# A last down projection of which 22 of 88 contraction tiles are made, two by two, by seven products of sums in place of eight, with their weight blocks on GpSimd's queue

## The chip, the cores and the metric

The kernel runs on one core of one Trainium2 chip. The metric is the time of one execution on the device in microseconds (us). A core has TensorE (PE, matrix products out of SBUF into PSUM), VectorE (DVE), ScalarE (ACT), GpSimd (POOL) and SyncE (SP), each with its own stream of instructions, and 16 DMA engines, for which SP, ACT and POOL issue transfers on a queue each.

## What is computed

A decoder trunk on one sequence of 256 tokens and 2048 features: a conformer convolution layer with its SwiGLU, a layer of dilated attention with its SwiGLU, and a final normalisation. The change touches only the end:

```python
h = h + _swiglu(_rmsnorm(h, ffn_norm_g[layer]), ffn_w_gate[layer], ffn_w_up[layer], ffn_w_down[layer])
return _rmsnorm(h, final_norm_g)      # (silu(x @ w_gate) * (x @ w_up)) @ w_down, w_down: 5632 x 2048, float32
```

## The kernel before

All work is on tiles of 128 partitions. Activations stand transposed (features on partitions, 256 tokens along the row), `hT` holds the residual. Each weight is float32 and each float32 product is made as three products of a faster type: a weight block is split into `whi` (a rounded copy, ScalarE, line 176) and `wlo` (the rest, VectorE, line 178), each activation likewise, and high x high, high x low and low x high are added up in PSUM.

Weight blocks of 512 KB come in the order of the list `blocks`. `next_block` (line 183) hands out the next one and first writes the instructions of the blocks up to two ahead (`emit_block`, line 153): the load into one of three `raw` buffers on SP's queue (line 173), then copy and subtraction into one of four `whi` and four `wlo` buffers. The order of instructions on each engine is laid out by a planner from the written order and the times that it expects; `later(n, fn)` writes `fn` after n further blocks, counted by `tick`.

The last down projection (lines 730 to 788) is token-major: `project_nat` (line 293) takes for each of four column blocks c (512 columns) the 22 blocks of 2 contraction tiles each. A block is multiplied with two halves of the tokens (t = 0, 1; 128 each), which are the stationary operand, the weights the moving one: 2 x 2 x 3 = 12 matmuls of 128 x 512, into one PSUM bank for each t. PSUM has eight banks: `pp` is two pairs, `aux` three banks, `one` one bank. During the first eight blocks of the stage `turn_over` (line 742) transposes the residual with `ident` (a part of the constants in `cst`), and ScalarE copies it into `hn`. At the end of a column block `add` (line 753) adds it to the residual and sums the squares, GpSimd multiplies by the gain. In the last column block the last three blocks are taken first for t = 0, then for t = 1, so that `done` (line 772: root, reciprocal, scaling and stores of the output) of the first half of the tokens runs beside the products of the second.

Of the kernel before, what the change touches and what calls it, by code (L numbers as in the profile page):

```python
# [9 lines left out]
F32 = mybir.dt.float32  # L10
F32R = mybir.dt.float32r
AF = mybir.ActivationFunctionType
ALU = mybir.AluOpType
# [3 lines left out]
P = 128  # L17
# [17 lines left out]
NATIVE = 4  # L35

TAPS_OF = [(6, 0)] * 14 + [(6, 6), (3, 16)]


_VEC = {}  # L40
# [39 lines left out]
def trunk(ctx: ExitStack, tc: tile.TileContext, xT, vec, const, w1, w2, wk, wv, wq, wo, wg0, wu0, wd0, wg1, wu1, wd1, fing, out):  # L80
# [34 lines left out]
    def new_x(pool, name, n=DT):  # L115

        return pool.tile([P, n, 2, S], F32R, name=name)
# [4 lines left out]
    def plan(w, u, kt_n, gk=GK):  # L122
        blocks.extend((w, u, g, gk) for g in range(kt_n // gk))
# [9 lines left out]
    for wg, wu, wd in ((wg0, wu0, wd0), (wg1, wu1, wd1)):  # L133
        for u in range(FT // 2):
            plan(wg, u, DT)
            plan(wu, u, DT)
        if wd is wd1:
            for c in range(D // NBV):
                plan(wd, c, FT, GKV)
# [10 lines left out]
    conv_pool = []  # L150
   

    def emit_block():
        i = len(ready)
        w, u, g, gk = blocks[i]
# [24 lines left out]
        if with_x and g == DT // GK - 1:  # L180
            x_loaded()

    def next_block(w, u, g, ahead=AHEAD):
        i = used[0]
        used[0] += 1
        assert blocks[i][:3] == (w, u, g)
        while len(ready) < min(len(blocks), i + 1 + ahead):
            emit_block()
        return ready[i]
# [42 lines left out]
    def bank2():  # L232
        return psum[-1].tile([P, 2, 2, S], F32, name="pp", bufs=2)

    def aux(shape):
        return psum[-1].tile(shape, F32, name="aux", bufs=3 if len(psum) > 1 else 5)
# [53 lines left out]
                                             skip_group_check=True)  # L290
                yield

    def project_nat(w, c, x, kt_n=DT, done=None):


        n = kt_n // GKV
        held = AHEAD + 1 if done else 0
        if done:
            outs = [aux([P, NBV]) for _ in range(2)]
        else:  # L300
            bk = bank2()
            outs = [bk[:, t, :, :].rearrange("p a b -> p (a b)") for t in range(2)]

        def tiles(hi, lo, g, j, t):
            kt = g * GKV + j
            o = outs[t]
            ts = slice(t * P, (t + 1) * P)
            nc.tensor.matmul(o, x[:, kt, 0, ts], hi[:, j, :], start=kt == 0, stop=False)  # L308
            nc.tensor.matmul(o, x[:, kt, 0, ts], lo[:, j, :], start=False, stop=False)  # L309
            nc.tensor.matmul(o, x[:, kt, 1, ts], hi[:, j, :], start=False, stop=kt == kt_n - 1)  # L310

        for g in range(n - held):
            hi, lo = next_block(w, c, g)[1:]
            for j in range(GKV):
                for t in range(2):
                    tiles(hi, lo, g, j, t)
            tick()
        last = []
        for t in range(2) if done else ():
            for g in range(n - held, n):  # L320
                if t == 0:
                    last.append(next_block(w, c, g)[1:])
                for j in range(GKV):
                    tiles(*last[g - n + held], g, j, t)
            done(t, outs[t])
        return outs

    def collect(bk, pool, name, bufs):
# [401 lines left out]
    with tc.tile_pool(name="ff", bufs=1) as ff:  # L730
        hid = ffn_hidden(ff, wg1, wu1, x, norm)
        table(AF.Sqrt, silu[-1])

        both = new_x(rp, "x").bitcast(F32).rearrange("p t a s -> p (t a s)").rearrange("p (i t n) -> p i t n", i=2, t=2)
        hn, on = both[:, 0, :, :], both[:, 1, :, :]
        ss = [little("ss", 8) for t in range(2)]
        gain = []
        for c in range(D // NBV):
            gain.append(ff.tile([P, 2, S], F32, name="t", bufs=4).rearrange("p a b -> p (a b)"))
            nc.scalar.dma_start(gain[c], fing[:, c * NBV:(c + 1) * NBV])  # L740

        def turn_over(i, t):

            pt = aux([P, 4, P])
            for a in range(4):
                nc.tensor.transpose(pt[:, a, :], hT[:, 4 * i + a, t * P:(t + 1) * P], ident)
            nc.scalar.copy(hn[:, t, 4 * i * P:4 * (i + 1) * P], pt.rearrange("p a b -> p (a b)"))

        for i in range(DT // 4):
            for t in range(2):  # L750
                later(2 * i + t, lambda i=i, t=t: turn_over(i, t))

        def add(c, t, p):

            cs = slice(c * NBV, (c + 1) * NBV)
            nc.vector.tensor_tensor(out=hn[:, t, cs], in0=p, in1=hn[:, t, cs], op=ALU.add)
            nc.vector.scalar_tensor_tensor(out=on[:, t, cs], in0=hn[:, t, cs], scalar=1.0, in1=hn[:, t, cs], op0=ALU.mult, op1=ALU.mult,
                                           accum_out=ss[t][:, c:c + 1])
            if c < D // NBV - 1:
                nc.gpsimd.tensor_tensor(out=on[:, t, cs], in0=hn[:, t, cs], in1=gain[c], op=ALU.mult)  # L760

        for c in range(D // NBV - 1):
            bk = project_nat(wd1, c, hid, FT)
            for t in range(2):
                add(c, t, bk[t])

        for t in range(2):
            r = ss[t][:, 4:5]
            nc.vector.tensor_reduce(out=r, in_=ss[t][:, 0:3], axis=AX.X, op=ALU.add)
            nc.vector.tensor_scalar(out=r, in0=r, scalar1=1.0 / D, scalar2=RMS_EPS, op0=ALU.mult, op1=ALU.add)  # L770

        def done(t, p):
            c = D // NBV - 1
            add(c, t, p)
            r = ss[t][:, 5:6]
            nc.scalar.activation(r, ss[t][:, c:c + 1], AF.Sqrt, scale=1.0 / D, bias=ss[t][:, 4:5])
            nc.vector.reciprocal(r, r)
            for i, eng in ((0, nc.scalar), (2, nc.vector), (1, nc.scalar), (3, nc.vector)):
                cs = slice(i * NBV, (i + 1) * NBV)
                if i == c:  # L780
                    nc.vector.scalar_tensor_tensor(out=on[:, t, cs], in0=hn[:, t, cs], scalar=r, in1=gain[c], op0=ALU.mult, op1=ALU.mult)
                elif eng is nc.scalar:
                    nc.scalar.activation(on[:, t, cs], on[:, t, cs], AF.Identity, scale=r)
                else:
                    nc.vector.tensor_scalar(out=on[:, t, cs], in0=on[:, t, cs], scalar1=r, scalar2=None, op0=ALU.mult)
                (nc.scalar if eng is nc.scalar else nc.sync).dma_start(out[t, :, cs], on[:, t, cs])

        project_nat(wd1, D // NBV - 1, hid, FT, done)


def _rows(a):
# [44 lines left out]
```

## Time and profile before

| what | value |
|---|---|
| median of 3 runs | 2182.6 us (2182.5 to 2182.79) |
| profiled execution: its own time | 2182.09 us |
| profiled execution: span from first to last instruction | 2180.3 us |
| granted TensorE clock, mean | 0.998 of full speed |
| TensorE busy | 2161.6 us (99% of the span) |
| last down projection on TensorE | from 1929.47 us to the last matmul at 2172.47 us |

A line of the timeline gives start, duration, engine, line of the kernel, operation, and the tiles written and read. Matmuls are pipelined: a duration reaches past the start of the next one, so what one costs is read from start to start. PE and PEld are matmul and the load of the stationary operand, which overlap. A buffer number is left out of a tile's name.

### The profile page before, as it was taken

The numbers are of one execution on the slowest core, as the hardware profiler recorded it, in microseconds if no ns is written. First come the engines' busy times: TensorE is split into PE (matmuls) and PEld (weight loads), VectorE is DVE, ScalarE is ACT, GpSimd is POOL, SyncE is SP. The second block draws the span as 40 slices with busy tenths as digits, with TensorE's granted clock in tenths as the row PEclk, the third lists the DMA queues.
The fourth block names the chain that finished last, engine by engine and source line by source line (L and its number), as shares of the span: only waits on it lengthen the run. The fifth ranks groups of instructions, "written<-read, shape, count | busy, mean of one in ns | idle before, by whom it ended". The sixth has DMA issues, their size and how long they took to land.

```text
span 2180.3 us, 31164 instructions
## 1 busy us (share of the span) xinstructions
PE 2161.6 (99%) x12254; PEld 1904.8 (87%) x12254; DVE 1327.9 (61%) x1636; ACT 1063.1 (49%) x1385; POOL 418.2 (19%) x284
## 2 busy tenths in 40 slices
PE   9999899999999999999999999999999999999998
PEld 8999788888888888888888888888888888888887
DVE  6888866555555554555545777665555555545554
ACT  6665555444444443444444566454444444453333
POOL 5998111111121210000000100012121111200000
PEclk9999999999999999999999999999999999999999
DMA  7444355555555555555565544555555555565564
GB/s 248 175 167 162 106 194 183 190 187 193 192 187 191 186 192 190 188 193 192 184 193 191 188 143 146 177 191 186 190 188 191 192 189 188 193 198 192 194 193 160
DMA packets 112899, 402.42 MB, mean 185 GB/s; under 512 B 12656, under 2 KB 13680, under 8 KB 112752
## 3 DMA queue, kind: packets, MB, share of 16 engines
q1 hardware_dynamic: 111456, 398.30, 55.1%
q8 instruction: 96, 1.57, 0.3%
q10 hardware_dynamic: 1296, 2.12, 0.3%
q14 instruction: 51, 0.42, 0.1%
HBM read 398.28 MB, written 2.10 MB: 184 GB/s over the span
## 4 chain that ended last, share of the span: by engine, by line
PE 97%; DVE 1%; DMA 1%; ACT 0%; issue 0%; POOL 0%; SPq 0%; ACTq 0%; DVEq 0%; POOLq 0%
PE pp L222 47%; PE pp L226 25%; PE pp L264 7%; PE pp L308 4%; PE pp L310 4%; PE pp L309 4%; PE aux L310 1%; PE aux L308 1%; PE aux L309 1%; PE pp L289 1%; DMA raw<-w 0%; DVE aux L475 0%; PE pp L277 0%; PE aux L700 0%; PE aux L677 0%
## 5 line engine op out<-in xcount | busy, mean ns | idle before, releaser
L178 DVE TENSOR_TENSOR wlo<-raw,whi 128x1024 fp32r<-128x1024 f32 (+1 forms) x692 | 900.8, 1318 | 752.7 <-ACT whi L176 598.1
L176 ACT CAST whi<-raw 128x1024 fp32r<-128x1024 f32 (+1 forms) x737 | 771.1, 1048 | 951.6 <-PE pp L222 633.8
L222 PE MATMUL pp<-x,whi 128*128 128x512 f32 x3328 | 778.0, 390 | 0.0
L222 PEld LDWEIGHTS pp<-x,whi 128*128 128x128 f32 x3328 | 617.2, 188 | 123.4
L226 PEld LDWEIGHTS pp<-x,wlo 128*128 128x128 f32 x3328 | 414.2, 192 | 8.6
L226 PE MATMUL pp<-x,wlo 128*128 128x256 f32 x3328 | 418.6, 283 | 0.0
L222 PE MATMUL pp<-hid,whi 128*128 128x512 f32 x704 | 164.3, 390 | 0.0
L222 PEld LDWEIGHTS pp<-hid,whi 128*128 128x128 f32 x704 | 130.6, 188 | 26.1
L475 DVE SCALAR_TENSOR_TENSOR aux<-up,vecs,aux 128x256 f32<-128x256 f32 x350 | 140.9, 481 | 1.6 <-ACT aux L473 1.6
L655 POOL TENSOR_TENSOR hid<-t,hid 128x512 fp32r<-128x512 f32 x44 | 57.1, 1298 | 417.1 <-ACT hid L654 417.1
L264 PE MATMUL pp<-x,whi 128*128 128x256 f32 x720 | 133.5, 287 | 0.0
L360 POOL TENSOR_TENSOR sqacc<-sqacc,sq 128x512 f32<-128x512 f32 x22 | 29.5, 1343 | 516.3 <-ACT sq L356 506.1
L649 POOL TENSOR_TENSOR t<-t,rstd 128x512 f32<-128x512 f32 x44 | 57.1, 1298 | 344.3 <-DVE t L332 344.3
L264 PEld LDWEIGHTS pp<-x,whi 128*128 128x128 f32 x720 | 113.3, 192 | 0.9
L178 POOL TENSOR_TENSOR wlo<-raw,whi 128x1024 fp32r<-128x1024 f32 x45 | 107.2, 2407 | 21.3 <-ACT whi L176 21.3
L308 PE MATMUL pp<-whi,hid 128*128 128x512 f32 x264 | 103.5, 392 | 0.0
L310 PE MATMUL pp<-whi,hid 128*128 128x512 f32 x264 | 102.8, 390 | 0.0
L309 PE MATMUL pp<-wlo,hid 128*128 128x512 f32 x264 | 102.8, 389 | 0.0
L264 PE MATMUL pp<-x,wlo 128*128 128x256 f32 x360 | 101.8, 283 | 0.0
L331 ACT COPY t<-pp 128x512 f32<-128x512 f32 x104 | 61.2, 589 | 71.7 <-PE pp L222 71.7
L226 PEld LDWEIGHTS pp<-hid,wlo 128*128 128x128 f32 x704 | 87.6, 192 | 1.9
L226 PE MATMUL pp<-hid,wlo 128*128 128x256 f32 x704 | 88.2, 283 | 0.0
(156 smaller groups left out, 1960.1 us busy)
## 6 DMA issues: line engine op xcount, KB each, us to landing
raw<-wg SPq DMA_DIRECT2D x176, 512.0 KB, 3.3
raw<-wu SPq DMA_DIRECT2D x176, 512.0 KB, 3.3
raw<-wd SPq DMA_DIRECT2D x176, 512.0 KB, 3.9
raw<-w SPq DMA_DIRECT2D x75, 512.0 KB, 3.3
raw<-wv SPq DMA_DIRECT2D x32, 512.0 KB, 4.2
raw<-wk SPq DMA_DIRECT2D x32, 512.0 KB, 3.4
raw<-wq SPq DMA_DIRECT2D x32, 512.0 KB, 3.2
raw<-wo SPq DMA_DIRECT2D x32, 512.0 KB, 3.3
```

The costliest lines, as they stand in the source:

```text
L176: nc.scalar.copy(hi[:, part, :], raw[:, part, :])
L178: eng.tensor_tensor(out=lo[:, part, :], in0=raw[:, part, :], in1=hi[:, part, :].bitcast(F32), op=ALU.subtract)
L222: nc.tensor.matmul(bk[:, m, :, :], hi, x[:, k, :, :], start=k == 0, stop=k == kt_n - 1 and turned, skip_group_check=True)
L226: nc.tensor.matmul(bk[:, m, 0, :], lo, x[:, k, 0, :], start=False, stop=k == kt_n - 1 and not turned, skip_group_check=True)
L264: nc.tensor.matmul(bks[u][:, m, :], a[:, j, m * P:(m + 1) * P], b, start=kt == 0 and m == 0 and i == 0, stop=kt == DT - 1 and i == len(pas ...
L308: nc.tensor.matmul(o, x[:, kt, 0, ts], hi[:, j, :], start=kt == 0, stop=False)
L309: nc.tensor.matmul(o, x[:, kt, 0, ts], lo[:, j, :], start=False, stop=False)
L310: nc.tensor.matmul(o, x[:, kt, 1, ts], hi[:, j, :], start=False, stop=kt == kt_n - 1)
L331: nc.scalar.copy(t, bk[:, :, 1, :])
L475: nc.vector.scalar_tensor_tensor(out=acc[i % 2], in0=win, scalar=w, in1=acc[i % 2], op0=ALU.mult, op1=ALU.add)
L649: nc.gpsimd.tensor_tensor(out=t, in0=t, in1=_bc(norm.r, 2), op=ALU.mult)
L655: nc.gpsimd.tensor_tensor(out=hid[:, 2 * u:2 * u + 2, 1, :], in0=o, in1=hid[:, 2 * u:2 * u + 2, 0, :].bitcast(F32), op=ALU.subtract)
```

## The change

For 4 pairs of contraction tiles in the first half of the columns and 7 pairs in the second, the 2 x 2 products (two contraction tiles, two halves of the tokens, two column blocks) are made as seven products of sums in place of eight (Winograd's form). Two column blocks ("half") are now worked on together: `ITEMS` lists for each half the steps, "n" for two plain blocks (one for each column block), "S" for a pair made by sums. An S takes four split blocks q0 to q3 of 6, 3, 6 and 6 matmuls: 21 in place of 24.

- The two weight blocks of an S are loaded on GpSimd's queue, one to `cst`, whose constants are no longer needed, the other in two halves to two buffers of tag `t`; the loads for the next S are written behind q3 of the one before (`load_sums`). They no longer go through `raw`.
- `emit_sums` makes four differences of half blocks on VectorE and splits seven half blocks (the two of q0 in one operation).
- `sum_up` makes the sums of the activations for seven pairs on VectorE and ScalarE, one at every third of the first blocks of the stage, into the space of the last `x`; two gain buffers serve as scratch, so the gains are loaded later, two at a time, on GpSimd's queue (before: four at the stage's beginning on ScalarE's).
- The plain products gather in the four banks of `aux` and `one`, four products of sums in the four of `pp`; `combine` adds these to the residual after the last S of a half, five operations on VectorE, one on ScalarE and three on GpSimd.
- The residual is turned over in place in `hT`, by way of two of the `pp` banks. The output is written to `raw` buffers and stored from there.

The core of the diff (the removed lines stand in the listing above):

```diff
+SUMS = 7
+ITEMS = "n" * 8 + "Snn" * 3 + "Sn" + "nnn", "nnn" + "SnnSnSn" * 2 + "Sn" + "nnn"
...
+    def load_sums(n):
+        if n < len(all_sums):
+            half, u = all_sums[n]
+            src = [wd1[2 * half + i, u].rearrange("p (k n) -> p k n", k=GKV) for i in range(2)]
+            nc.gpsimd.dma_start(cst.rearrange("p (k n) -> p k n", k=GKV), src[0])
+            for i in range(2):
+                nc.gpsimd.dma_start(halves[i], src[1][:, i, :])
...
+        def parts(i, raw):
+            nc.scalar.copy(hi[:, i, :], raw)
+            nc.vector.tensor_tensor(out=lo[:, i, :], in0=raw, in1=hi[:, i, :].bitcast(F32), op=ALU.subtract)
...
+        if q == 0:
+            nc.scalar.copy(hi, first_raw[0])
+            nc.vector.tensor_tensor(out=lo, in0=first_raw[0], in1=hi.bitcast(F32), op=ALU.subtract)
+            t1 = difference(b12, b11, "sq")
+            t3 = difference(b22, b12, "sq")
+            t2 = difference(b22, t1, "sqacc")
+            first_raw.extend((t1, t2, difference(b21, t2, "sqacc"), t3))
+        elif q == 1:
+            parts(1, b22)
+        elif q == 2:
+            parts(0, first_raw[1])
+            parts(1, first_raw[2])
+        else:
+            parts(0, first_raw[4])
+            parts(1, first_raw[3])
+            load_sums(all_sums.index((half, u)) + 1)
...
+        later(n, lambda: load_sums(0))
...
+        def sum_up(u):
+            h, d = gain[0].rearrange("p (a b) -> p a b", b=S), wide(gain[1])
+            two = hid[:, 2 * u:2 * u + 2, :, :].bitcast(F32)
+            nc.vector.tensor_tensor(out=h, in0=two[:, :, 0, :], in1=two[:, :, 1, :], op=ALU.add)
...
+            for i, a, b, op in ((0, a21, a22, ALU.add), (1, d[:, 0, :], a11, ALU.subtract), (2, a11, a21, ALU.subtract),
+                                (3, a12, d[:, 1, :], ALU.subtract)):
+                nc.vector.tensor_tensor(out=d[:, i, :], in0=a, in1=b, op=op)
+            nc.scalar.copy(sums[:, u, :, 0, :], d)
+            nc.vector.tensor_tensor(out=sums[:, u, :, 1, :], in0=d, in1=sums[:, u, :, 0, :].bitcast(F32), op=ALU.subtract)
+        for u in range(SUMS):
+            later(2 + 3 * u, lambda u=u: sum_up(u))
...
+            uses = (((ps[0], tokens(hid, k, 0), 0), (cs[0][0], tokens(hid, k + 1, 0), 1)),
+                    ((cs[0][1], two[3], 1),),
+                    ((ps[1], two[0], 0), (ps[2], two[1], 1)),
+                    ((ps[3], two[2], 0), (cs[1][0], tokens(hid, k + 1, 1), 1)))
+            for q, use in enumerate(uses):
+                hi, lo = next_block("sums", (half, u), q)[1:]
+                for o, xs, j in use:
+                    nat(o, xs, hi[:, j, :], lo[:, j, :], start and any(o is p for p in ps))
+                tick()
...
+            nc.scalar.copy(u2, p1)
+            plus(r[0][0], p1)
+            plus(u2, p6)
+            nc.vector.tensor_tensor(out=u3, in0=p7, in1=u2, op=ALU.add)
+            plus(r[0][1], p5)
+            plus(r[1][1], p5)
+            for o, a in ((r[0][1], u2), (r[1][0], u3), (r[1][1], u3)):
+                nc.gpsimd.tensor_tensor(out=o, in0=a, in1=o, op=ALU.add)
```

## Rows read from the trace of the kernel before

**Rows 1.** The profile's page: its first line, the busy time of each engine with its share of the span and count of instructions, and the shares of the chain that ended last, by engine.

```profile
span 2180.3 us, 31164 instructions
...
PE 2161.6 (99%) x12254; PEld 1904.8 (87%) x12254; DVE 1327.9 (61%) x1636; ACT 1063.1 (49%) x1385; POOL 418.2 (19%) x284
...
PE 97%; DVE 1%; DMA 1%; ACT 0%; issue 0%; POOL 0%; SPq 0%; ACTq 0%; DVEq 0%; POOLq 0%
```

**Rows 2.** The table of windows, core 0, two stretches of the last down projection (us from the span's start; busy us of each engine with its count of instructions, the granted TensorE clock, the DMA engines' share, GB/s).

```profile
1990.00:2050.00 60.00, 60.00 (x266) 49.70 (x265) 31.55 (x29) 23.21 (x22) 3.87 (x2) 1.00 0.58 193
2050.00:2112.00 62.00, 62.00 (x276) 51.32 (x275) 32.04 (x30) 24.27 (x23) 3.92 (x2) 1.00 0.60 191
```

**Rows 3.** TensorE's timeline in a block of steady state (start us, us, engine, line, operation), and the groups of its matmuls from 1929.4 us to the end (line, engine, tiles, form, count, busy us, mean ns of one, idle us before them).

```profile
2085.66 0.39 PE L308 MATMUL pp<-whi,hid 128*128 128x512 f32 x1
...
2088.38 0.39 PE L308 MATMUL pp<-whi,hid 128*128 128x512 f32 x1
...
L308 PE MATMUL pp<-whi,hid 128*128 128x512 f32 x264 | 103.5, 392 | 0.0
L310 PE MATMUL pp<-whi,hid 128*128 128x512 f32 x264 | 102.8, 390 | 0.0
L309 PE MATMUL pp<-wlo,hid 128*128 128x512 f32 x264 | 102.8, 389 | 0.0
...
L308 PE MATMUL aux<-whi,hid 128*128 128x512 f32 x88 | 34.2, 389 | 0.0
L309 PE MATMUL aux<-wlo,hid 128*128 128x512 f32 x88 | 34.2, 389 | 0.0
L310 PE MATMUL aux<-whi,hid 128*128 128x512 f32 x88 | 34.2, 389 | 0.0
```

**Rows 4.** The timelines of ScalarE and VectorE in steady state (in brackets the idle time before an instruction and what ended it), the waits of the SP queue from 1925 us on, and one of the waits of all engines from 1760 us on (who waited for whom: us in total, times, longest).

```profile
2107.62 1.05 ACT L176 CAST whi<-raw 128x1024 fp32r<-128x1024 f32 x1 [1.67 <-PE pp L310]
...
2105.99 1.22 DVE L178 TENSOR_TENSOR wlo<-raw,whi 128x1024 fp32r<-128x1024 f32 x1 [1.50 <-ACT whi L176]
...
SPq L173 <- DVE wlo L178: 190.2, 82, 6.4
...
ACT whi L176 <- DMA raw<-wd: 0.4, 1, 0.4
```

**Rows 5.** VectorE's timeline: three whole-block subtractions in a row, two operations on half tiles in a row, and two half-tile operations of which the second needs the first; then line 686's accumulating products on 128 and 256 columns (ns: least, median, most).

```profile
1935.78 3.61 DVE L178 TENSOR_TENSOR wlo<-raw,whi 128x1024 fp32r<-128x1024 f32 x3 [4.00 <-ACT whi L176]
...
2113.06 1.29 DVE L756 TENSOR_TENSOR x<-pp,x 128x512 f32<-128x512 f32 x2 [0.41 <-PE pp L310]
...
2172.90 0.69 DVE L756 TENSOR_TENSOR x<-aux,x 128x512 f32<-128x512 f32 x1 [0.87 <-PE aux L310]
2173.62 0.69 DVE L757 SCALAR_TENSOR_TENSOR x<-x 128x512 f32<-128x512 f32 x1
...
L686 DVE SCALAR_TENSOR_TENSOR e<-e,cst x32: 286/358/426, 1253.8 to 1354.2; 128x128 f32<-128x128 f32 x16, 128x256 f32<-128x256 f32 x16
```

**Rows 6.** The issues of loads (tile and source, queue, count, KB each, median us from issue to landing), and a window of 10 us of the stage (busy us of the instructions on raw, clock, DMA share, GB/s).

```profile
raw<-wd SPq DMA_DIRECT2D x176, 512.0 KB, 3.9
...
hT<-xT SPq DMA_DIRECT2D x6, 256.0 KB, 6.0
...
t<-fing ACTq DMA_DIRECT2D x4, 256.0 KB, 4.0
...
cst<-const SPq DMA_DIRECT2D x1, 512.0 KB, 6.3
...
2000.00:2010.00 10.00, 5.16 (x5) 3.46 (x4) 0.00 (x0) 1.00 0.74 239
```

**Rows 7.** The timelines of ScalarE and TensorE at the beginning of the stage, where the first pieces are turned over.

```profile
1934.21 0.59 ACT L747 COPY x<-aux 128x512 f32<-128x512 f32 x1 [1.78 <-POOL hid L655]
1934.69 2.00 ACT L176 CAST whi<-raw 128x1024 fp32r<-128x1024 f32 x2
...
1932.20 0.60 PE L746 MATMUL aux<-cst,hT 128*128 128x128 f32 x4
...
1932.87 0.40 PE L309 MATMUL pp<-wlo,hid 128*128 128x512 f32 x1
...
1934.95 0.39 PE L309 MATMUL pp<-wlo,hid 128*128 128x512 f32 x1
```

**Rows 8.** The timelines of GpSimd and VectorE at the end of the third column block, and the durations of a like GpSimd operation elsewhere (ns: least, median, most).

```profile
2115.04 3.91 POOL L760 TENSOR_TENSOR x<-x,t 128x512 f32<-128x512 f32 x2 [55.92 <-DVE x L757]
...
2115.55 2.24 DVE L178 TENSOR_TENSOR wlo<-raw,whi 128x1024 fp32r<-128x1024 f32 x1
...
L655 POOL TENSOR_TENSOR hid<-t,hid x44: 1287/1296/1310, 348.0 to 1932.5; 128x512 fp32r<-128x512 f32 x44
```

**Rows 9.** The timeline from the last matmul on, and the stores' times to landing.

```profile
2171.62 0.96 ACTq L786 DMA_DIRECT2D out<-x  x2
...
2172.47 0.39 PE L310 MATMUL aux<-whi,hid 128*128 128x512 f32 x1
...
2174.88 1.33 ACT L783 ACTIVATE x<-x,ss 128x512 f32<-128x512 f32 x2 [0.23 <-DVE ss L777]
2174.96 0.49 DVE L785 TENSOR_SCALAR x<-x,ss 128x512 f32<-128x512 f32 x1
...
out<-x ACTq DMA_DIRECT2D x4, 256.0 KB, 2.8
```

More of the change, by code (lines that the diff above doesn't have):

```diff
@@ L185, in next_block @@
         used[0] += 1
-        assert blocks[i][:3] == (w, u, g)
+        assert blocks[i][:3] == (w, u, g) or (w == "sums" and blocks[i] == (w, *u, g))
         while len(ready) < min(len(blocks), i + 1 + ahead):
@@ new lines, in trunk, with residual_of, wide, turn_over @@
+        buf = [ff.tile([P, 2, S], F32, name="t", bufs=4).rearrange("p a b -> p (a b)") for _ in range(4)]
+        halves.extend(buf[0:2])
+        gain = buf[2:4]
+        def residual_of(c, t):
+            return hT[:, 4 * c:4 * c + 4, t * P:(t + 1) * P]
+        def wide(a):
+            return a.rearrange("p (a b) -> p a b", b=P)
+        def turn_over(c, t, b):
+            for a in range(4):
+                nc.tensor.transpose(wide(b)[:, a, :], hT[:, 4 * c + a, t * P:(t + 1) * P], ident)
+            nc.scalar.copy(residual_of(c, t), wide(b))
@@ new lines, in trunk, with load_gain, plus, seven @@
+        for u in range(SUMS):
+            later(2 + 3 * u, lambda u=u: sum_up(u))
+        def load_gain(half):
+            for i in range(2):
+                c = 2 * half + i
+                nc.gpsimd.dma_start(gain[i], fing[:, c * NBV:(c + 1) * NBV])
+        later(3 * SUMS + 2, lambda: load_gain(0))
+        def plus(o, p):
+            nc.vector.tensor_tensor(out=o, in0=p, in1=o, op=ALU.add)
+        def seven(half, u, cs, ps, start):
+            k = 2 * u
+            two = [[sums[:, u, i, j, :] for j in range(2)] for i in range(4)]
+            uses = (((ps[0], tokens(hid, k, 0), 0), (cs[0][0], tokens(hid, k + 1, 0), 1)),
[7 more added lines that the diff above has]
+                tick()
@@ L758, in add @@
                                            accum_out=ss[t][:, c:c + 1])
             if c < D // NBV - 1:
[L760 to L770, printed above, removed]
+                nc.gpsimd.tensor_tensor(out=h, in0=h, in1=wide(gain[c % 2]), op=ALU.mult)
@@ new lines, in done, with plain @@
+                (nc.scalar if eng is nc.scalar else nc.sync).dma_start(out[t, :, i * NBV:(i + 1) * NBV], y)
+        for half, items in enumerate(ITEMS):
+            n_sums = items.count("S")
+            last_sum = items.rindex("S")
+            u_sums, u_plain = iter(range(n_sums)), iter(range(n_sums, FT // GKV))
+            cs, ps = first if half == 0 else (plain_banks(), sum_banks())
+            begun = [False, False]
+            if half:
+                load_gain(half)
+            def plain(i, u, stop, ts=(0, 1), parts=None):
+                hi, lo = parts or next_block(wd1, 2 * half + i, u)[1:]
+                for j in range(GKV):
+                    for t in ts:
+                        nat(cs[t][i], tokens(hid, u * GKV + j, t), hi[:, j, :], lo[:, j, :], not begun[i] and j == 0, stop and j == GKV - 1)
+                begun[i] = True
+            ahead = [next(u_plain) for _ in range(2)]
+            for i in range(2):
+                for u in ahead:
+                    plain(i, u, False)
+                    tick()
+            for n, k in enumerate(items[2:-3]):
+                if k == "S":
+                    u = next(u_sums)
+                    seven(half, u, cs, ps, u == 0)
+                    if n + 2 == last_sum:
+                        combine(half, ps)
+                else:
+                    u = next(u_plain)
+                    for i in range(2):
+                        plain(i, u, False)
+                        tick()
+            rest = list(u_plain)
+            for i in range(2):
+                c = 2 * half + i
+                if c < D // NBV - 1:
+                    for u in rest:
+                        plain(i, u, u == rest[-1])
+                        tick()
+                    for t in range(2):
+                        add(c, t, cs[t][i])
+                    continue
+                for t in range(2):
+                    r = ss[t][:, 4:5]
+                    nc.vector.tensor_reduce(out=r, in_=ss[t][:, 0:3], axis=AX.X, op=ALU.add)
+                    nc.vector.tensor_scalar(out=r, in0=r, scalar1=1.0 / D, scalar2=RMS_EPS, op0=ALU.mult, op1=ALU.add)
+                held = []
+                for t in range(2):
+                    for n, u in enumerate(rest):
+                        if t == 0:
+                            held.append(next_block(wd1, c, u)[1:])
+                        plain(i, u, u == rest[-1], (t,), held[n])
+                    done(t, cs[t][i])
```

117 lines of the change are left out of this document (69 added, 48 removed).

## The prediction

> **What bounds the kernel now.** Read first the page's busy shares and its chain of waits: TensorE is busy 2161.6 of 2180.3 us, and 97% of the chain that ended last is its matmuls [rows 1]. Then the table of windows over the last down projection: TensorE fills every window, VectorE is busy 53%, ScalarE 39%, and the DMA engines move 193 GB/s at a share of 0.58 [rows 2]. Then the price of one matmul, which is not its duration: the table of groups has 389 to 392 ns, but those overlap. The timeline has the same line at 2085.66 and at 2088.38 with eleven matmuls between, so one costs 2.72/12 = 0.2267 us [rows 3], and a block of twelve 2.72 us. No group of these matmuls has idle time before it [rows 3]: TensorE waits for nobody here, and what is taken off it comes off the time as long as that stays so.
>
> How far the others are from stalling it: in steady state ScalarE copies a block in 1.05 us after waiting 1.67 us for TensorE to give back a buffer, then VectorE subtracts in 1.22 us after waiting 1.50 us for ScalarE [rows 4]. So the split is held back only by the four buffers of whi and wlo: it is done 0.2 + 1.05 + 1.22 = 2.5 us after the release, and its block is due three blocks, 8.2 us, after it. The SP queue waits for VectorE to free raw buffers, 190 us in all, and ScalarE waited for a block of the down projection only 0.4 us [rows 4]: loads are not the limit either.
>
> **The change part by part.**
>
> *The products.* Half 0 has 4 places with S, half 1 has 7: 11 places, at each of which two blocks of 12 matmuls become 6+3+6+6 = 21. That is 33 matmuls fewer, all on the path: 33 x 0.2267 = **7.48 us**. Nothing else of TensorE changes (the 32 transposes stay).
>
> *VectorE at an S.* It now subtracts one whole block, four half-tile differences, and five half-tile splits. Back to back, whole ones step at (3.61 - 1.23)/2 = 1.19 us, half ones at 1.29 - 0.69 = 0.60 us, and one that needs the result before it at 0.72 us [rows 5]. An S costs 1.19 + 8 x 0.60 + 0.72 = 6.7 us of VectorE against 21 x 0.2267 = 4.76 us of TensorE: inside an S it is the slower one, and the plain blocks around it (2 x 1.19 against 5.44) must give the time back. With one pair of plain blocks between two S the cycle is 9.1 us of VectorE in 10.20 us of TensorE, with two pairs 11.5 in 15.64. I follow the tight cycle, S starting on TensorE at 0: q0 ends at 1.36, q1 2.04, q2 3.40, q3 4.76, the plain blocks 7.48 and 10.20. A buffer is free 0.2 us after the end of the block four earlier. The copy and split of q0 can start at -6.6, its split ends at -4.35, the four differences at -1.8, q1's split at -1.2, q2's at 0.0 (due 2.04), q3's at 2.0 (its buffer comes at 0.2; due 3.40), the plain ones at 3.8 (due 4.76) and 5.0 (due 7.48). The thinnest margin is 1 us, and each cycle starts 0.35 us later than the one before; only two tight gaps follow each other. So no stall, at 0.2 us for the steps; if each operation took its full 1.23 and 0.69 us without overlap, the cycle is 9.9 us, which still fits.
>
> *The blocks by GpSimd's queue.* Three loads (512, 256, 256 KB) for each S. They wait for the last difference (-1.8) and, the third, for q1's split (-1.2). Behind them on GpSimd stand only the three adds of a half's end, the gain loads and the products with gain. The first load waits for the last transpose with ident (tick 8), still six blocks, 16 us, ahead of q0. The trace has no load from this queue: its price is bounded. Let L be the time from the last difference to the landing of all three. ScalarE's copy of q0 and VectorE's differences wait for the landing, and in order behind them every split up to the next plain blocks, for which TensorE waits. From the landing VectorE needs three differences (1.9 us) to the last one, then 0.6 + 1.2 + 1.2 + 1.2 to the split of the first plain block, due at 10.20 + 4.76 + 0.2; so the halves may land 9.1 after the S start; from an S that follows two pairs (its last difference at -3.2) two tight gaps in a row allow 2L + 1.9 <= 9.1 + 10.2 + 3.2, so **L up to 10.3 us is free**. Half 1 has two such runs, so each us beyond costs 2 x 2 = 4 us. Low end for L: streamed at 239 GB/s, the highest rate that I found in a window of the stage, 1.05 MB take 4.4 us, and the latency on top, 3.9 us for a raw block less its 2.2 us of streaming, is 1.7: 6.1 us. High end: each as slow as the slowest loads of the trace and one after another, 6.3 + 6.0 + 6.0 = 18.3 us [rows 6]. I take the middle road that the share gives: 239 GB/s at 0.74 is a capacity of some 323 GB/s; half of it for this queue while SP's also runs makes 6.5 + 1.7 = **8.2 us**, nearest to the raw rows because the same engines carry both. So nothing is lost. The Trainium skill, "DMA: Bandwidth & Descriptors", section "Anatomy of one DMA — SWDGE (gpsimd) path", fits such a load as 2.0 us plus bytes over 436 GB/s; by that, as an estimate, L is 4.4 us if the fixed parts overlap and 8.4 us if they don't, and the sum stays.
>
> *The rest.* SP issues 66 blocks in place of 88, and ScalarE's queue no longer the four gain loads (256 KB, 4.0 us); both are relieved. The seven sum_up cost VectorE 2 x 0.60 + 4 x 0.29 = 2.4 us each, 17 us over the first 22 blocks (some 60 us), where VectorE has 1.5 us idle in every 2.72. Their inputs are old, so they fit the gaps; but the last three come at ticks 14, 17 and 20, where the first S (block 16) starts. If VectorE and ScalarE keep the written order, ScalarE's copy for a sum stands before the copy of the next block and waits 2.4 us for VectorE, and the first S loses up to 3 us. The trace shows that the order is not the written one: the copy L747 of a turned-over piece runs at 1934.21 before the block copies at 1934.69 that stand ahead of it in the code [rows 7]. I take **+0.3**, ends 0 and 3. *combine*, once a half: five VectorE operations of 0.60 to 0.72 (3.2 us) after q3, then three GpSimd adds. While GpSimd runs such an add, VectorE's subtraction takes 2.24 us in place of 1.23 [rows 8]. From 5.0 on: combine to 8.4, the next split with the lock to 10.6 where it is due by 10.4; the following ones catch up. I take **+0.3 for each half**, ends 0 and 1.6 each. The adds at the ends of column blocks stay as they were (TensorE waited for none of them, [rows 3]). *The tail*: the same operations in the same order from the last matmul on [rows 9]; the output now goes through raw buffers, three for four tiles, so the fourth waits until ScalarE's first two stores have landed (issued at 2171.6 to 2172.6, 2.8 us, so about 2175.4, where VectorE wrote at 2174.96); it stays behind ScalarE's last store: **+0.1**, ends 0 and 0.5. Turning over hT in place costs nothing more; among its transposes nine matmuls take 2.08 us, 0.231 each [rows 7]; over the 96 of these blocks that is 0.4 us, which could vanish.
>
> *Sum* against the profiled execution, 2182.09 us with its span of 2180.3: -7.48 + 0.3 + 0.6 + 0.1 = -6.5, so 2175.6; the median of the runs, 2182.6, is 0.5 above it, so **2176.1 us** (-0.30%).
>
> **The rivals.**
>
> (A) GpSimd's queue is late. For it: no row of this queue, the high end of 18.3 us, and VectorE, which stands in order behind the landing, has only 1 us of margin. Against it: the DMA engines have 40% free. It decides from L = 10.3 us on and eats the whole gain at 10.3 + 6.5/4 = 11.9 us; at 13 us the loss is 4 x 2.7 = 10.8, so 2187; at 18.3 us 32, so 2208. TensorE would then wait at q0 and q1 of the second and third S of each tight run. Chance 0.20, of which 0.12 past the point where it is slower than before by over 0.2%.
>
> (B) VectorE and GpSimd lock each other out also when GpSimd issues loads. By [rows 8] a GpSimd operation costs VectorE 1.0 us. Three a cycle make 9.1 + 3.0 = 12.1 us in 10.20: 1.9 us lost in each of the four tight gaps, 7.7 in all, so 2183.8: no difference. Against it: a load reads no tile through GpSimd. Chance 0.13. The Trainium skill, "SBUF — State Buffer", section "SBUF: two separate sides", tells of the same port the other way round: descriptors of GpSimd's loads starve while VectorE holds the shared port in its two-port modes; its section "Who interferes with whom" adds that subtractions of two tensors have no such mode and, as an inference, leave the descriptors alone. The trace has no load of GpSimd's and shows neither; by the first sentence the loads would be late (A), by the second neither happens.
>
> (C) The sums are made in the written order: the first S loses 3 us, the time is 2178.8: no measurable difference. Chance 0.10.
>
> **How the numbers follow.** What a measurement of this kernel can tell from no change is about 0.2%, 4.4 us: faster means below 2178.2, slower above 2187.0. The forecast has 0.57 and lies wholly in faster, 2174.6 (the lowest run, 2182.5, less 7.48 and the 0.4 of the turned-over blocks, with no stall) to 2178.1. Same: 0.08 of A, B and C, 0.31. Slower: 0.12 of A. The range for 8 in 10 goes from 2174.6 over B and C to 2185.0 and leaves out the far part of A.
>
> **What would show it.** Right: 1023 in place of 1056 matmuls in the stage, stepping at 0.2267; no wait of TensorE over 0.7 us; raw and GpSimd loads landing within 8 us of their issue; VectorE about 85% busy in the runs of S with one pair between. The products' term is wrong if the matmuls step otherwise; the queue's if q0 or q1 wait for a load (A); VectorE's if they wait for wlo while the loads have long landed (B), or around the first S only (C). The forecast as a whole is wrong if the sum of TensorE's waits in the stage is over 3 us.

## The result and the profile after

The changed kernel takes **2189.97 us** (median of 6 runs, 2188.24 to 2193.26), the kernel before beside it 2182.55 us (6 runs, 2182.31 to 2182.83): ratio 1.0037, 95% interval 1.0024 to 1.005. It is slower by 7.4 us, where a gain to 2176.1 us was forecast, with a range of 2174.6 to 2185.0. The profiled execution took 2189.8 us, with a span of 2188.0.

The page first, in the lines that answer to [rows 1]: span, busy times, and the shares of the chain that ended last.

```profile
span 2188.0 us, 31353 instructions
...
PE 2159.7 (99%) x12221; PEld 1898.0 (87%) x12221; DVE 1399.0 (64%) x1776; ACT 1085.8 (50%) x1438; POOL 449.3 (21%) x327
...
PE 87%; issue 5%; DVE 4%; DMA 2%; POOL 1%; ACT 1%; SPq 0%; DVEq 0%; POOLq 0%; ACTq 0%
```

TensorE's share still rounds to 99%, but the chain now leaves it: 97% has become 87%, and VectorE, the DMA engines and GpSimd stand in it. The same two windows as [rows 2] show where:

```profile
1990.00:2050.00 60.00, 58.52 (x255) 47.21 (x254) 44.08 (x54) 28.58 (x35) 11.07 (x12) 1.00 0.60 195
2050.00:2112.00 62.00, 58.63 (x253) 46.94 (x253) 48.24 (x58) 27.50 (x36) 14.35 (x18) 1.00 0.54 186
```

TensorE (first pair of numbers) filled both windows before and now leaves 1.48 and 3.37 us empty, with VectorE (third) 73% and 78% busy. The table of waits from 1925 us on (who waited for whom: us in total, times, longest) names the parties:

```profile
DVE sq L200 <- DMA cst<-wd: 21.2, 8, 3.7
...
PE aux L367 <- DVE wlo L249: 5.1, 8, 0.7
...
PE pp L367 <- DVE wlo L196: 3.6, 4, 1.4
...
DVE sq L200 <- issue: 2.2, 1, 2.2
```

TensorE waits for nobody's load. It waits for VectorE's splits, at the fourth block of a pair (q3, line 196) and at the first plain block behind it (line 249); and VectorE waits for a load eight times, up to 3.7 us, at line 200, the first difference of the *next* pair. A ninth such wait, 2.2 us, has no releaser in the table ("issue"), but there too the difference starts within 0.1 us of its load's landing: 23.4 us in nine waits, of which the first, 1.6 us, stands ahead of the first pair. VectorE's timeline over one such place, with the idle time and its cause in brackets:

```profile
2095.46 0.69 DVE L200 TENSOR_TENSOR sqacc<-cst,sqacc 128x512 f32<-128x512 f32 x1
2096.06 0.69 DVE L196 TENSOR_TENSOR wlo<-t,whi 128x512 fp32r<-128x512 f32 x1
2096.81 0.69 DVE L196 TENSOR_TENSOR wlo<-sq,whi 128x512 fp32r<-128x512 f32 x1
2097.42 0.69 DVE L196 TENSOR_TENSOR wlo<-sqacc,whi 128x512 fp32r<-128x512 f32 x1
2101.59 0.69 DVE L200 TENSOR_TENSOR sq<-t,cst 128x512 f32<-128x512 f32 x1 [3.48 <-DMA cst<-wd]
2102.31 0.69 DVE L200 TENSOR_TENSOR sqacc<-t,sq 128x512 f32<-128x512 f32 x1
2102.92 0.69 DVE L196 TENSOR_TENSOR wlo<-sq,whi 128x512 fp32r<-128x512 f32 x1
2103.53 0.68 DVE L196 TENSOR_TENSOR wlo<-sqacc,whi 128x512 fp32r<-128x512 f32 x1
2104.13 0.69 DVE L200 TENSOR_TENSOR sq<-t 128x512 f32<-128x512 f32 x1
2104.73 2.35 DVE L249 TENSOR_TENSOR wlo<-raw,whi 128x1024 fp32r<-128x1024 f32 x2
```

From the timeline of all engines over the same, the lines of GpSimd, ScalarE and TensorE that the reading needs:

```profile
2096.69 0.53 POOL L182 DMA_DIRECT2D cst<-wd  x1 [3.72 <-DVE sqacc L200]
...
2099.40 0.61 ACT L195 CAST whi<-sqacc 128x512 fp32r<-128x512 f32 x1
...
2102.08 0.39 PE L366 MATMUL pp<-whi,sums 128*128 128x512 f32 x1
2103.66 0.50 PE L367 MATMUL pp<-wlo,sums 128*128 128x512 f32 x1 [1.20 <-DVE wlo L196]
...
2104.92 0.39 PE L366 MATMUL aux<-whi,hid 128*128 128x512 f32 x1
2106.01 0.50 PE L367 MATMUL aux<-wlo,hid 128*128 128x512 f32 x1 [0.69 <-DVE wlo L249]
```

Read them together. The last difference of a pair (2095.46) frees `cst`, into which the next pair's first block is loaded; the issue starts at 2096.69, and the load lands by 2101.59. At 2098.11 VectorE has done q2's splits, and next in its order stands not q3's split but the next pair's first difference, `sq<-t,cst`. It waits 3.48 us for the landing, and q3's splits wait behind it, though from 2100.01 on, when ScalarE's second copy for them has ended, both have their data. TensorE needs the first at 2102.08 + 0.2267 = 2102.31 and gets it at 2103.66; the plain block behind is late by the same queue.

The sum: over the stage TensorE's steps are 12.6 us longer than 0.2267 us each (of steps over by more than 0.1; the waits of the table, 8.7, are shorter than what the steps lose, as in the step 2102.08 to 2103.66, 1.35 over with a wait of 1.20). The stage ran from 1929.47 to 2172.47 before, 243.0 us, and from 1930.70 to 2179.24 after, 248.5: 12.6 - 7.48 = 5.1 of the 5.5 between them. The tail is 2188.0 - 2179.24 = 8.76 in place of 7.83. The rest, 1.23 us, lies ahead of the stage in code that the change doesn't touch; the experiments' stages begin between 1930.0 and 1931.6, so they differ by more than that among themselves, but all begin later than the one profile of the kernel before; what makes it stays open. 5.54 + 0.93 + 1.23 = 7.7, the spans' difference.

The loads that this queue had no row for (answers to [rows 6]: from 1925 us on, tile and source, queue, count, KB, median us to landing):

```profile
raw<-wd SPq DMA_DIRECT2D x63, 512.0 KB, 4.2
t<-wd POOLq DMA_DIRECT2D x22, 256.0 KB, 3.8
cst<-wd POOLq DMA_DIRECT2D x11, 512.0 KB, 4.5
```

The tail's timeline, answering to [rows 9]:

```profile
2179.24 0.39 PE L368 MATMUL b<-whi,hid 128*128 128x512 f32 x1
...
2182.79 0.49 DVE L904 TENSOR_SCALAR raw<-hT,ss 128x512 f32<-128x512 f32 x1 [1.16 <-DMA out<-raw]
```

### The profile page after: what moved, and what is told of

It is laid out like the page before. It is cut to its first block, busy times and chain, and to the rows that moved or that the text cites. A ratio compares the mean times of both kernels' runs of the same rounds, so it can differ in the third digit from the quotient of the medians.

```text
span 2188.0 us, 31353 instructions
## 1 busy us (share of the span) xinstructions
PE 2159.7 (99%) x12221; PEld 1898.0 (87%) x12221; DVE 1399.0 (64%) x1776; ACT 1085.8 (50%) x1438; POOL 449.3 (21%) x327
## 3 DMA queue, kind: packets, MB, share of 16 engines
q8 instruction: 95, 1.56, 0.3%
## 4 chain that ended last, share of the span: by engine, by line
PE 87%; issue 5%; DVE 4%; DMA 2%; POOL 1%; ACT 1%; SPq 0%; DVEq 0%; POOLq 0%; ACTq 0%
PE pp L293 47%; PE pp L297 25%; PE pp L335 7%; PE pp L366 1%; PE pp L368 1%; PE pp L367 1%; DVE wlo L249 1%; DMA cst<-wd 1%; PE pp L360 1%; PE aux L367 1%; PE aux L368 0%; DMA raw<-w 0%; PE aux L366 0%; PE pp L348 0%; DVE aux L533 0%
## 5 line engine op out<-in xcount | busy, mean ns | idle before, releaser
L249 DVE TENSOR_TENSOR wlo<-raw,whi 128x1024 fp32r<-128x1024 f32 (+1 forms) x670 | 874.1, 1324 | 658.5 <-ACT whi L247 504.0
L247 ACT CAST whi<-raw 128x1024 fp32r<-128x1024 f32 (+1 forms) x715 | 746.9, 1048 | 881.0 <-PE pp L293 626.6
L367 PE MATMUL aux<-wlo,hid 128*128 128x512 f32 x220 | 86.6, 394 | 5.1 <-DVE wlo L249 5.1
L366 PE MATMUL aux<-whi,hid 128*128 128x512 f32 x220 | 86.4, 393 | 0.0
L368 PE MATMUL aux<-whi,hid 128*128 128x512 f32 x220 | 85.8, 390 | 0.0
```

The source lines that it names most:

```text
L366: nc.tensor.matmul(o, xs[0], hi, start=start, stop=False, skip_group_check=True)
L367: nc.tensor.matmul(o, xs[0], lo, start=False, stop=False, skip_group_check=True)
L368: nc.tensor.matmul(o, xs[1], hi, start=False, stop=stop, skip_group_check=True)
```

## The experiments

Three theories at first. **ORDER**: the landing itself is early enough; what costs is the place of the next pair's first difference in VectorE's order, ahead of splits that are ready. **QUEUE**: loads by GpSimd's queue land too late, whatever stands where. **CAPACITY**: VectorE has too much to do in a tight cycle (an S and one pair of plain blocks), whatever the order. All ratios are to the kernel before.

**1. The order alone (e1_order).** The loads stay; the differences are queued behind the six splits emitted last, which is the written order.

```diff
+            with ExitStack() as st:
+                for ins in last_lo[-6:]:
+                    st.enter_context(tc.issue_after(ins))
                 t1 = difference(b12, b11, "sq")
```

> Three theories. ORDER: VectorE's stream has the first differences of the next pair ahead of this pair's q3 splits and of the plain splits behind them, so those stand behind the landing of the next load; that makes the 12.6 us by which TensorE's steps exceed 0.2267 us in the profile of the changed kernel. CAPACITY: VectorE has too much to do in a cycle of one S and one pair of plain blocks (9.1 us of 10.2 by my count), whatever the order. QUEUE: loads on GpSimd's queue come too late, whatever stands behind them. Here the four differences are only queued behind the splits that stand before them in the code; loads, queue and work are the same. ORDER: TensorE's excess in the stage falls below 2 us, the time to 2177 to 2179 us (7.5 us of products less 1 us of the tail and the 1.2 us by which the stage already starts later). CAPACITY: excess stays over 8 us, time over 2186. QUEUE: the waits move from q3 to q0 and q1 and stay over 6 us in all, time over 2184.

Measured: 2177.12 us (2175.23 to 2178.58), ratio 0.9971, 0.996 to 0.9983. TensorE has no wait in the stage, which takes 2167.16 - 1931.64 = 235.5 us: 7.5 less than before. The loads land about as in the changed kernel (4.6 and 3.4 us). VectorE's timeline, two tight cycles:

```profile
2089.39 1.22 DVE L206 TENSOR_TENSOR wlo<-cst,whi 128x1024 fp32r<-128x1024 f32 x1
2090.53 0.68 DVE L201 TENSOR_TENSOR sq<-t,cst 128x512 f32<-128x512 f32 x1
...
2096.14 0.69 DVE L197 TENSOR_TENSOR wlo<-sqacc,whi 128x512 fp32r<-128x512 f32 x1
2097.31 2.36 DVE L253 TENSOR_TENSOR wlo<-raw,whi 128x1024 fp32r<-128x1024 f32 x2 [0.49 <-ACT whi L251]
2099.59 1.22 DVE L206 TENSOR_TENSOR wlo<-cst,whi 128x1024 fp32r<-128x1024 f32 x1
2100.72 0.68 DVE L201 TENSOR_TENSOR sq<-t,cst 128x512 f32<-128x512 f32 x1
```

The difference now stands behind the plain splits and q0's split and waits for nothing; the cycle is 10.20 us, TensorE's own. The windows of that run:

```profile
2050.00:2112.00 62.00, 62.00 (x275) 51.38 (x274) 51.33 (x63) 31.08 (x39) 12.94 (x17) 1.00 0.63 206
2060.00:2150.00 90.00, 90.00 (x399) 74.55 (x398) 73.87 (x96) 48.24 (x63) 12.20 (x21) 1.00 0.59 195
```

TensorE is full again at a higher VectorE share (83% and 82%) than the changed kernel has: it is not VectorE's amount of work that costs (CAPACITY).

**2. The queue alone (e2_sp_queue).** The order is left to the planner; the three loads go on SP's queue.

```diff
-            nc.gpsimd.dma_start(cst.rearrange("p (k n) -> p k n", k=GKV), src[0])
+            nc.sync.dma_start(cst.rearrange("p (k n) -> p k n", k=GKV), src[0])
```

> The loads of the pairs are issued on SP's queue in place of GpSimd's; VectorE's order is nearly that of the changed kernel. QUEUE: the waits go, time 2177 to 2179 us. ORDER: VectorE still stands in front of the landing, which comes 3.9 in place of 4.5 us after the issue and later still where SP waits for something else first: excess 8 to 14 us, time 2187 to 2192. CAPACITY: as ORDER.

Measured: 2182.83 us (2181.3 to 2185.27), ratio 0.9999, 0.9989 to 1.0008: between both numbers, and neither theory had it. The landings are the same (4.6 and 3.9 us). Its waits:

```profile
DVE sq L200 <- issue: 8.6, 5, 2.3
DVE sq L200 <- DMA cst<-wd: 8.1, 4, 2.8
...
PE aux L367 <- DVE wlo L249: 4.2, 7, 0.7
```

The difference still waits nine times (of the five put down to "issue", too, four end 0.08 us behind the landing in `cst`, the fifth 0.4), but for 16.7 us in place of 23.4, and the waits at q3 are gone. Two things moved. In three tight gaps SP's issue starts 0.03 to 0.06 us after the last difference has ended, where GpSimd's started 0.54 after it, and the landing comes 4.6 to 5.0 us after that difference in place of 5.3 to 5.5. And the planner's order differs: in two places (after 2091.8 and 2130.9) q3's splits now precede the second difference, and in one (after 2103.0) all four. So this edit moved the order along with the landing, and doesn't tell the two apart.

**3. No landing to wait for (e3_load_once).** Only the first pair is loaded, and the other products are made of its weights; the order on VectorE stays nearly that of the changed kernel.

```diff
-            load_sums(all_sums.index((half, u)) + 1)
+            pass
```

> Only the first pair's blocks are loaded, ten of eleven loads are left out, and the other pairs use the first one's blocks (so these products are of the wrong weights). VectorE's order stays as in the changed kernel, with nothing to wait for. ORDER: excess under 3 us (two operations ahead of q3's splits still cost 1.2 us each time against a margin of 1.4), time 2177 to 2180 us. QUEUE: the same. CAPACITY: excess over 8 us, time over 2186.

Measured: 2176.27 us (2176.01 to 2178.42), ratio 0.9972, 0.996 to 0.9983, no wait of TensorE in the stage. The order costs nothing without a landing to wait for, and by run 1, in which nothing less is loaded, a landing of some 5 us costs nothing in another order: it takes both.

**4. Half of the order (e6_behind_q3).** The differences are queued behind q3's two splits, but not behind the plain ones.

```diff
+                for ins in q3_lo[-2:]:
+                    st.enter_context(tc.issue_after(ins))
```

> Half of e1_order's edit: the differences of the next pair are queued behind this pair's q3 splits, but not behind the plain splits; one of them still stands ahead of those and waits there for the landing. In the changed kernel five operations of 0.6 us stand between the landing and the end of the first plain split's queue; here it is one. ORDER: no wait at q3; the first plain block's wait shrinks from 0.85 us to under 0.3 each, excess under 3 us, time 2177 to 2180. If any wait of VectorE for the landing were enough, the plain blocks' 0.85 us would stay at seven to eight places: excess 6 to 7 us, time 2183 to 2185.

Measured: 2180.1 us (2178.67 to 2182.95), ratio 0.9988, 0.9979 to 0.9998. VectorE's timeline at one of two places, TensorE's there, and TensorE's waits:

```profile
2109.25 0.69 DVE L203 TENSOR_TENSOR sq<-t,cst 128x512 f32<-128x512 f32 x1 [2.34 <-DMA cst<-wd]
2109.86 3.49 DVE L255 TENSOR_TENSOR wlo<-raw,whi 128x1024 fp32r<-128x1024 f32 x3
```

```profile
2111.13 0.50 PE L373 MATMUL aux<-wlo,hid 128*128 128x512 f32 x1 [1.28 <-DVE wlo L255]
```

```profile
PE aux L373 <- DVE wlo L255: 1.7, 2, 1.3
```

The waits move with the difference: those at q3 are gone, those at the plain block remain in two places, behind differences that waited 2.34 and 1.50 us, and cost 2.3 us of step in all in place of 12.6. The recorded "under 0.3 each" missed (1.44 and 0.60 us of step), and the time is 0.1 us above its range. This tells the mechanism best: TensorE waits just at the splits that stand behind the waiting difference.

**5. The tail (e5_order_tail, e5b_order_tail, e4_tail).** The first output tile goes into `cst`, idle by then, so that no store is waited for. e5 and e5b are the same kernel, with the order of run 1; e4 has the planner's order.

```diff
-            o = [wp.tile([P, GKV, NBV], F32, name="raw", bufs=RAW) for _ in range(2)]
+            o = [cst.rearrange("p (k n) -> p k n", k=GKV) if t == i == 0 else wp.tile([P, GKV, NBV], F32, name="raw", bufs=RAW) for i in range(2)]
```

> e1_order, and the first of the four output tiles goes to the space of cst in place of a raw buffer, so that no tile waits for a store. If the wait of VectorE's last scaling for a store is what makes the tail 0.9 us longer than before, this is 0.9 to 1.1 us below e1_order; if not, within 0.3 us of it.

> e5_order_tail again, with more rounds and beside e7_more_sums: 2175.8 us as before.

> The changed kernel as it is, with only the first output tile moved to the space of cst. The tail is 0.9 to 1.1 us shorter, the stage stays: 2188 to 2190 us, with the same 12 us of excess. If the tail hung together with the waits of the stage, the change would be larger.

Measured: 2175.77 us (0.9968, 0.9955 to 0.9981) and 2176.09 (0.9968, 0.9956 to 0.9981) beside 2177.12 for run 1; e4 2190.11 (1.0032, 1.002 to 1.0044). The wait for the store is gone in all three, and the tails are 8.49, 8.6 and 8.49 us, where run 1 has 8.94 and the changed kernel 8.76: 0.3 to 0.5 us, not the 0.9 to 1.1 that was expected. By the traces' landings the last store lands 6.92 us after the last matmul in e4, as in the kernel before, and 7.16 after it in the changed kernel; from that landing to the span's end it is 1.56 us in e4 and e5, 1.63 in the changed kernel and 0.90 before. So most of the 0.93 us by which the tail grew isn't the store's wait. The times alone don't show a gain this small.

**6. The changed kernel again (e11_changed_again)**, as a measure for the last.

> The changed kernel once more, on the chip and beside the runs of this call, as the measure of how far its runs differ among themselves. 2188 to 2193 us; TensorE's waits in the stage 11 to 14 us. The run with the tail alone changed (2190.1 us) can be told from it only if this one comes out above 2191 us.

Measured: 2191.22 us (2189.61 to 2191.84), ratio 1.0037, 1.0022 to 1.0051; TensorE's steps are 14.2 us too long, 12.6 in the first profile. e4's interval overlaps with this one: what the tail alone gives stays unproven by times.

**7. More of it (e7_more_sums, e10_more_sums_b).** Order and tail as in e5, and 14 pairs by sums in place of 11; e10 puts a plain pair between the last sum of half 0 and the closing blocks.

```diff
-SUMS = 7
-ITEMS = "n" * 8 + "Snn" * 3 + "Sn" + "nnn", "nnn" + "SnnSnSn" * 2 + "Sn" + "nnn"
+SUMS = 8
+ITEMS = "n" * 7 + "Sn" * 6 + "nnn", "nnn" + "Sn" * 8 + "nnn"
```

> e5_order_tail with 14 places in place of 11 (6 in the first half, 8 in the second, eight sums), all but one with a single pair of plain blocks between. ORDER: with nothing out of order the tight cycle of 9.1 to 9.3 us of VectorE fits 10.20 of TensorE for any length of run, so nine more matmuls go: 9 x 0.2267 = 2.0 us, 2173.7. CAPACITY: each cycle begins some 0.3 us later than the one before (my walk), which a run of eight does not forgive: waits of 1 to 3 us, time 2174.5 to 2177.

> Order and output tile as in the run of 2176.1 us, with 14 pairs by sums in place of 11, as in the run of 2175.4 us, but with one pair of plain blocks between the last pair by sums of the first half and the blocks that close it. If the 1.05 us that TensorE waited there came from VectorE's five operations of the half's end right ahead of the closing blocks' splits, the wait is gone: 2174.0 to 2175.0 us. If not, 2175.4 us as before, with a wait somewhere else.

Measured: e7 2175.36 us (0.9964, 0.9952 to 0.9977), with one wait of TensorE, 0.72 us at 2059.62 (1.15 us of step); e10 **2173.98 us** (2172.49 to 2174.74; 0.9958, 0.9945 to 0.9971), with none. e7's time lies in CAPACITY's range, but its wait doesn't lie in a run of pairs: it is in the first plain blocks of half 1, where VectorE's split stands behind the four operations that add up a column block (from 2054.84), 23 us after half 0's *combine* (2033.92 to 2036.9). So that *combine* made it, as e10's expectation supposes, isn't shown, though e10 is without it. Three pairs more are 9 matmuls fewer, 9 x 0.2267 = 2.0 us; e10's stage is 2.0 us shorter than e5b's (233.5 in place of 235.5), its time 2.1. It is the fastest version of the study, and a run of eight tight cycles without a wait speaks against CAPACITY once more. Its long run of tight cycles:

```profile
2060.00:2150.00 90.00, 90.00 (x398) 74.53 (x398) 79.43 (x104) 50.01 (x67) 16.30 (x24) 1.00 0.58 192
```

**8. A later landing (e8_changed_twice, e9_order_twice).** The 512 KB load is issued twice; the second overwrites the first, so it starts when that has landed. e8 leaves the order to the planner, e9 has that of run 1.

```diff
-            nc.gpsimd.dma_start(cst.rearrange("p (k n) -> p k n", k=GKV), src[0])
+            for _ in range(2):
+                nc.gpsimd.dma_start(cst.rearrange("p (k n) -> p k n", k=GKV), src[0])
```

> The changed kernel, but the 512 KB load of each pair is issued twice, so that its landing comes later. The planner that orders the instructions counts with the later landing and in most places puts the next pair's first difference behind the q3 splits of this pair, in some also behind the plain splits. Theory ORDER (what costs is that a difference waits for the landing ahead of splits that are ready): although more is loaded, it is not slower than the changed kernel, 2178 to 2190 us, and the q3 waits of TensorE are mostly gone. Rival QUEUE (what costs is the queue itself): slower than the changed kernel, above 2191 us.

> The run with the differences queued behind the last six splits (2177 us), but the 512 KB load of each pair is issued twice. The three loads then take about 10 us from the last difference to the landing in place of about 5.4, near the 10.3 us up to which the prediction's walk of VectorE in that order finds the landing free. Theory ORDER with that walk: TensorE's waits in the stage are 0 to 4 us, 2176 to 2181 us. Rival (the landing counts even behind the splits): each us of the 5 added costs one in each of the ten gaps between pairs, over 15 us of waits in all, above 2190 us.

Measured: e8 2202.27 us (2198.79 to 2204.27), ratio 1.0089, 1.0073 to 1.0105; e9 2199.04 us (2197.03 to 2203.17), 1.0076, 1.0062 to 1.009. ORDER missed both, and the rivals' numbers came in: order makes a landing of 5 us free, not one of 11, and so late a landing costs in either order. In e8 the planner did put the difference behind q3 (so its order depends on when it expects the landing), but often ahead of the plain splits; VectorE's timeline and TensorE's waits:

```profile
2001.00 0.69 DVE L201 TENSOR_TENSOR sq<-t,cst 128x512 f32<-128x512 f32 x1 [3.89 <-DMA cst<-wd]
2001.61 3.49 DVE L250 TENSOR_TENSOR wlo<-raw,whi 128x1024 fp32r<-128x1024 f32 x3
```

```profile
PE aux L368 <- DVE wlo L250: 12.1, 6, 2.8
```

In e9 (GpSimd's, VectorE's, ScalarE's and TensorE's timelines of one gap, and a window behind it):

```profile
2099.91 0.69 DVE L202 TENSOR_TENSOR sqacc<-cst,sqacc 128x512 f32<-128x512 f32 x1
```

```profile
2100.89 0.53 POOL L184 DMA_DIRECT2D cst<-wd  x1
2105.41 0.53 POOL L184 DMA_DIRECT2D cst<-wd  x1 [3.98 <-DMA cst<-wd]
```

```profile
2095.28 1.05 ACT L206 CAST whi<-cst 128x1024 fp32r<-128x1024 f32 x1 [5.37 <-DMA cst<-wd]
2112.26 1.04 ACT L206 CAST whi<-cst 128x1024 fp32r<-128x1024 f32 x1 [9.11 <-DMA cst<-wd]
```

```profile
2113.36 0.79 PE L373 MATMUL pp<-whi,hid 128*128 128x512 f32 x1 [3.66 <-ACT whi L206]
...
2115.64 0.63 PE L373 MATMUL aux<-whi,hid 128*128 128x512 f32 x1
...
2118.62 0.63 PE L373 MATMUL pp<-whi,sums 128*128 128x512 f32 x1
```

```profile
2114.00:2119.00 5.00, 4.53 (x11) 3.51 (x11) 5.00 (x9) 3.40 (x6) 1.62 (x3) 0.50 0.23 63
```

From the last difference's end, 2100.60, to ScalarE's copy of the landed block, 2112.26, are 11.7 us; over the gaps in which the copy waits it is 9.9 to 12.0. In half 1 TensorE's waits at q0 lie at the second and third pair of its tight runs, the places that rival A named. From a landing to the last difference it takes 2100.60 - 2095.28 = 5.3 us. Also the matmuls behind a wait of 3.66 us run at half speed: seven steps from 2115.64 to 2118.62, 0.426 us each, with a granted clock of 0.50 in the window. The doubled load also adds traffic for the other blocks (SP's raw loads land in 4.3 us in place of run 1's 4.1, between 1990 and 2150 us), so the run doesn't price the landing by itself.

## Why the prediction was wrong

**The step that failed** is the walk of VectorE's tight cycle, and with it the sentence on the queue that rests on it, "nothing is lost". The walk set VectorE's operations in written order: the next pair's differences behind this pair's q3 splits, the plain splits and its own q0 split. On the chip the first of them ran ahead of q3's splits in nine of the ten gaps (in eight the second one too); the tenth lies between the halves. That the planner doesn't keep the written order was in the prediction itself [rows 7], but it was used only where it helped, against rival C. The prediction did see that splits stand "in order behind" the landing; but it took the first plain block behind the *following* pair for the split that has to be on time (due at 15.16 in its clock, so that the halves might land 9.1 after the S start), where the splits that suffered were this pair's q3, due at 3.40, and the plain block behind it, due at 4.76. The cost is 12.6 us against 0.

**The landing** was mis-sized, but on the safe side. In the order that the walk took, which run 1 has, all three loads have landed 4.5 to 5.1 us after the last difference in the ten gaps, below the low end of 6.1; in the changed kernel the waiting difference starts 5.4 us after it (2095.46 + 0.69 = 2096.15 to 2101.59). The Trainium skill, "DMA: Bandwidth & Descriptors", section "Anatomy of one DMA — SWDGE (gpsimd) path", gave, as an estimate, 4.4 us with the fixed parts side by side; the traces are nearer to that than to my 8.2.

**The free limit of 10.3 us** was too wide. It gave 1.9 us from the landing to the last difference; run 8 shows 5.3, since in this order ScalarE's copy and q0's split come first, and a split of q1 stands among the differences. With 2L + 5.3 in place of 2L + 1.9 under the same 22.5 us, L may be 8.6, an estimate that no run tested by itself.

**Products**: right. Run 1's stage is 7.5 us shorter (7.48).

**First S, combine**: 0.3 and 0.6 were set aside; runs 1 and 3 have no wait at either, and the changed kernel has none before 1997.

**Tail**: 0.1 us, ends 0 and 0.5; it is 0.93 longer. The wait for a store came, 1.16 us on VectorE, and put off the last store's landing by 0.24 us, within the ends. The other 0.7 us lies between that landing and the span's end, where the sum had no term; runs without the store's wait have it too (1.56 us in e4, 0.90 before), e10 hardly (0.96), so its cause stays open.

**Rivals.** A had the right parties, a difference behind a landing, and the wrong condition: it was to decide from L = 10.3 on, at q0 and q1. TensorE lost time at L = 5.4, at q3 and the plain block. B is refuted: VectorE's half subtraction at 2096.81 takes 0.69 us beside a load's issue on GpSimd at 2096.69, and so it is throughout: 22 half-tile operations beside such an issue took 0.68 to 0.69 us, 76 others 0.68 to 0.70. C did not happen. **What would show it** worked as written: waits over 3 us mean that the forecast as a whole is wrong; but "VectorE's if they wait for wlo while the loads have long landed" did not cover a split that waits for a load which it doesn't use.

## What to carry to other kernels

On an engine that works in order, an operation that waits for a transfer costs what stands behind it, whether or not that needs the transfer: when a change adds one, walk the engine in the order that will really run, and price the landing for each place where the operation could stand. Where a planner orders the work, its choice is an unknown to be bounded like a duration; here the two orders lie 13 us apart, more than the whole gain. If ready work stands behind a wait, an explicit order behind that work is a cheap cure (2189.97 to 2177.12 us), and with it the stage saves the forecast 7.48 us in full, as long as the landing is not much later than the 5 us of this case (run 8).

## What was not expected of the hardware

- From the issue on, GpSimd's queue delivers nearly as fast as SP's: 4.5 us for 512 KB beside 4.2, with 0.53 us of issue on GpSimd for each load, and 4.6 and 3.9 us for the pair's loads when they go on SP's queue (run 2). But in tight gaps GpSimd began the issue 0.54 us after the operation that it waited for, SP 0.03 to 0.06.
- After some of the long waits TensorE's steps were 0.426 us in place of 0.2267, at the lower of its two clock levels (granted 0.50, 1.2 GHz), for several us (run 8, behind a wait of 3.66 us); in the changed kernel, whose waits reach 1.4 us, the clock stayed at 1.00 in both windows. Such a wait is thus dearer than its own length. The length alone doesn't decide it: in e8 a wait of 1.82 us (to 2100.55) was followed by steps of 0.426 us, one of 2.77 us (to 2002.88) was not.
